# Two raw tiles of their own for the conditioning loads during the first FFN's output products

## The chip, the cores and the metric

One Trainium2 chip, one of its cores. The metric is the device time of one execution in microseconds (us); lower is better. TensorE (PE) does the matrix products, VectorE (DVE) and ScalarE (ACT) the elementwise work, GpSimd (POOL) a few reductions, SyncE (SP) issues most loads from device memory.

## The reference, cut to what matters

Two layers, S = 512 tokens, D = 1024, in float32. Each layer has a mixer and an FFN; the first layer's FFN is where this change lies.

```python
cond = jax.nn.silu(c)
for layer in range(DEPTH):
    mod = (cond @ ada_w[layer] + ada_b[layer])[:, None, :]
    sh1, sc1, g1, sh2, sc2, g2 = jnp.split(mod, 6, axis=-1)
    ...
    y = swiglu_ffn(u, ffn_w_in[layer], ffn_w_out[layer])   # (silu(gate) * up) @ w_out, w_out is 2816 x 1024
    h = h + (1.0 + g2) * rms_norm(y, norm_g[layer, 3])
```

The vector `mod` does not depend on the tokens. Its weights `ada_w` (1024 x 6144 for each layer) are read from device memory beside the FFN's own, and the kernel spreads that work over stretches in which PE is busy with something else.

## The kernel before

**Products.** A float32 operand is cut into a rounded part `hi` and a rest `lo`, and each product is three matmuls: hi by hi, hi by lo, lo by hi (`three`, lines 582, 583, 584). Weights come as float32 into a raw tile of 1 MB; ACT casts it to `hi` (line 96) and DVE subtracts to get `lo` (line 97).

**The stream.** All weights and all conditioning data go through one list of items in the order of their use (`Stream`). Each item has a kind: `"w"` (a weight to be cut), `"ada"` (1 MB of `ada_w`, which DVE multiplies by `cond` in four instructions, lines 398 and 400), `"rows"` (two 256 KB broadcasts of a bias and a gain, used at lines 447 and 448) or `"do"` (no load, only work). `fill` issues the loads of the next items, in the list's order, from the SP queue, as long as at most `raws` = 2 loaded items are not yet consumed. All of them take a tile with the tag `raw`, of which there are two, so a load waits on SP until the tile that it gets has been read for the last time, whether that was a weight or a conditioning item. SP is one queue: a load that waits holds up all behind it. `take` cuts weights up to two ahead of the one in use; three `hi`/`lo` pairs exist, so weight k can be cut once PE is done with weight k - 3.

**The first FFN's output products.** `ffn(0, ...)`: after the products by `ffn_w_in` (`seven_products`), `w_out` comes as 11 weights of 256 rows each, which this text numbers w0 to w10. One weight is two steps of 128 rows, and a step is 4 token tiles x 2 halves x 3 = 24 matmuls of 128x512. The left operand of each step is cut from the tile `mid` into `oh` and `ol` (lines 1063 and 1064, five buffers of each). Ten `ada` and two `rows` items are woven between the 11 weights. Item numbers run on through the kernel: w0, w1, w2, w3, w4, w5, w6 are `raw65`, `raw67`, `raw69`, `raw71`, `raw74`, `raw76`, `raw79`; `raw66`, `raw68`, `raw70`, `raw73`, `raw75`, ... are `ada`, `raw72` and `raw77` are `rows`. In the same stretch the rotary angles of the next layer are worked out (tiles `a0`, `a1`, `pos_i`). The steps w9 and w10 are used together, one token tile at a time, and then the next layer's attention begins.

**What sets the order.** Up to w8 the scheduler of the framework puts the instructions of each engine in an order of its own choice, from its own estimate of times; from w9 on the order is written by hand (`manual_schedule`). SP takes what the scheduler gives it.

**Sides.** Pools are stacked from the left or the right end of each partition. The tiles `th`, `tl` and `spare` of `seven_products` stand on the side opposite to `mid`; when they are given up, the pool `roll` (for `oh`, `ol`) is opened there.

Of the kernel before, what the change touches and what calls it, by code (L numbers as in the profile page):

```python
# [11 lines left out]
F32 = mybir.dt.float32  # L12
# [5 lines left out]
P = 128  # L18
# [27 lines left out]
class Stream:  # L46


    def __init__(self, nc, pool, items, raws, parts):
        self.nc, self.pool, self.items, self.raws, self.parts = nc, pool, items, raws, parts  # L50
        self.loaded = 0
        self.done = 0
        self.raw = {}
        self.ready = []
        self.wpos = [i for i, it in enumerate(items) if it[0] == "w"]
        self.taken = 0

    def _load(self, i):
        kind, src = self.items[i][:2]
        if src is None:  # L60
            self.raw[i] = None
            return
        t = self.pool.tile([P, 2048], F32, name=f"raw{i}", tag="raw", bufs=self.raws)
        if kind == "quarters":
            v = t.rearrange("p (q k b) -> p q k b", q=4, k=4)
            for k in (1, 2, 3, 0):
                self.nc.sync.dma_start(v[:, k], src[k % 2][:, k // 2 * 4:k // 2 * 4 + 4])
        elif kind == "rows":
            for k in range(2):
                self.nc.sync.dma_start(t[:, k * 512:(k + 1) * 512], src[k])  # L70
        elif isinstance(src, tuple):
            v = t.rearrange("p (s a b) -> p s a b", s=len(src), a=src[0].shape[1])
            for k, s in enumerate(src):
                self.nc.sync.dma_start(v[:, k], s)
        else:
            self.nc.sync.dma_start(t.rearrange("p (a b) -> p a b", a=src.shape[1]), src)
        self.raw[i] = t

    def fill(self, most=99):
        real = lambda i: self.items[i][1] is not None  # L80
        while self.loaded < len(self.items) and sum(map(real, range(self.done, self.loaded))) + real(self.loaded) <= self.raws:
            if most == 0:
                return
            most -= 1
            self._load(self.loaded)
            self.loaded += 1
# [212 lines left out]
def block_kernel(tc, x, c, positions, ada_w, ada_b, norm_g, hgrn_w_in, lower, hgrn_norm_g, hgrn_w_out,  # L299
                 attn_w_in, attn_w_out, ffn_w_in, ffn_w_out, inv_freq, out):  # L300
    nc = tc.nc
    act, dve, pool, pe = nc.scalar, nc.vector, nc.gpsimd, nc.tensor
# [5 lines left out]
    with ExitStack() as ctx:  # L308
# [7 lines left out]
        def bank(tag):  # L316
            uid[0] += 1
            return psum.tile([P, 512], F32, name=f"ps_{tag}{uid[0]}", tag=tag, bufs={"mm": 4, "a": 2, "b": 2}[tag])
# [248 lines left out]
        st = Stream(nc, wp, items, 2, 3)  # L567
# [453 lines left out]
        def ffn(l, first, close, nxt, side):  # L1021
            turns.close()
            close()
            with ExitStack() as fx:
# [29 lines left out]
                    seven_products(range(2 * PLAIN[l], NF), mid, pss, spare, th, tl)  # L1054
                fl.drain()
                roll = fx.enter_context(tc.tile_pool(name=f"roll{l}", bufs=1, side=bass.opposite_side(side)))
                y0 = [bank("mm") for _ in range(NT)]
                y1 = [bank("a"), bank("b"), bank("a"), bank("b")]
                parts = {}
# [32 lines left out]
                def mm(t, ks=range(4)):  # L1092
                    for k in ks:
                        prods(t, NF - 4 + k, ws[k // 2], k % 2)

                def y_steps(t):
                    n.sq_y(t, 0)
                    n.sq_y(t, 1)
                    n.gated(t, 0)
                    n.r_y(t)  # L1100
                    n.gated(t, 1)
# [24 lines left out]
                with tc.manual_schedule(engines=ORDERED):  # L1126
                    mm(0)
                    y_steps(0)
                    n.upds(0)
                    n.r_h(0)  # L1130
                    n.xn(0)
                    mm(1)
                    y_steps(1)
                    n.upds(1)
                    mm(2, (0, 1))
                    n.flip(0, [bank("mm"), bank("a")])
                    n.u_of(0, 0)
                    n.u_of(0, 1)
                    n.r_h(1)
                    n.parts_of(0, 0)  # L1140
                    n.xn(1)
                    n.parts_of(0, 1)
                    mm(3, (0, 1))
                    for hi_f, lo_f in st.pieces(2, True):
                        hi_f()
                        lo_f()
                    st.fill()
                    mm(2, (2, 3))
                    y_steps(2)
                    n.upds(2)  # L1150
                    n.flip(1, [bank("mm"), bank("b")])
                    n.u_of(1, 0)
                    n.u_of(1, 1)
                    n.r_h(2)
                    n.parts_of(1, 0)
                    n.parts_of(1, 1)
                    n.xn(2)
                    mm(3, (2, 3))
                    y_steps(3)
                    fx.close()  # L1160
                    v_prod = nxt[1]()
                    vw = [st.take(0), st.take(0)]
                    v_prod(vw, 0, range(8))
                    n.upds(3)
                    n.flip(2, [bank("mm"), bank("a")])
                    n.r_h(3)
                    n.u_of(2, 0)
                    n.u_of(2, 1)
                    n.parts_of(2, 0)
                    n.parts_of(2, 1)  # L1170
                    n.xn(3)
                    v_prod(vw, 1, range(8))
                    n.flip(3, [bank("mm"), bank("b")])
                    n.u_of(3, 0)
                    n.u_of(3, 1)
                    n.parts_of(3, 0)
                    n.parts_of(3, 1)
                    for hi_f, lo_f in st.pieces(2, True):
                        hi_f()
                        lo_f()  # L1180
                    st.fill()
                    for t in range(NT):
                        act.dma_start(h_away[t], h[:, t])
                    v_prod(vw, 2, range(8))
                    v_prod(vw, 3, range(8))
# [469 lines left out]
        def open_attention():  # L1655
# [20 lines left out]
            return v_prod  # L1676

        ffn(0, first, h0.close, ((1, 0), open_attention), "right")
        v_away = dpool.tile([P, NT, 512], F32, name="v_away")

# [644 lines left out]
        made = aux, oh, ol, [b.t for b in y0], {0: y1[0].t}, [p.t for p in ws[2:]]  # L2325
        first = mixer_out(oT, store[0], gates.pop((1, 2)).t, 1, "left", cx.close, made)
        ffn(1, first, hx.close, None, "right")


# [29 lines left out]
```

## Time and profile before

| | us |
|---|---|
| median of 3 runs | 1475.56 (1474.87 to 1476.01) |
| the profiled execution, its own time | 1476.0 |
| its span, from the first to the last instruction | 1474.1 |
| PE busy | 1430.7 |
| first product by w0 | at 523.74 |
| second step of the tail (w9, second token tile) | at 633.02 |

Times in views of the trace are counted from the span's start. An entry in square brackets behind an instruction is the idle time of its engine ahead of it and who ended it. `SPq` rows are the issues of loads, not their transfers. A busy PE entry includes the modelled end of a matmul, so two neighbours overlap: the rate is read from starts.

### The profile page before, as it was taken

The page shows a single profiled execution, that of the slowest core. Times are in us where ns is not written, and L with a number is a line of the kernel's source. Part 1 is how long each engine was busy: PE and PEld are TensorE (multiplying, and loading weights), DVE is VectorE, ACT ScalarE, POOL GpSimd, SP SyncE. Part 2 cuts the span into 40 slices and gives each one's busy share as a digit, 9 for nine tenths or more (in the row PEclk, how much of TensorE's full clock was granted, in tenths as well). Part 3 has the DMA queues.
Part 4 walks back from the last instruction along what each step waited for, and adds up shares of the span by engine and source line. Part 5 has one row for each costly group of instructions (what it writes and reads, how often), then busy time and mean ns, then how long its engine had stood idle before and what let it go on. Part 6 is the DMA issues. An engine that isn't in the chain of part 4 may idle for free. (4 is left out here: it accounts for less than half of the span.)

```text
span 1474.1 us, 25335 instructions
## 1 busy us (share of the span) xinstructions
PE 1430.7 (97%) x9903; PEld 1312.5 (89%) x9903; DVE 1113.8 (76%) x1800; ACT 824.7 (56%) x1484; POOL 190.1 (13%) x173
## 2 busy tenths in 40 slices
PE   8999999999999999998999999999999999999998
PEld 6777888889999987787998999999998999999887
DVE  4588688488888876777788877788776978887644
ACT  4434442474555542267748778657896645555332
POOL 1011102031111100231000110001012211110100
PEclk9999999999999999999999999999999999999999
DMA  9656554223333355734244543254344233334541
GB/s 308 192 192 197 172 173 145 84 78 94 110 109 111 108 178 195 230 113 143 90 122 119 147 123 109 64 172 137 94 138 149 86 104 112 110 110 149 191 143 58
DMA packets 212872, 201.10 MB, mean 136 GB/s; under 512 B 8920, under 2 KB 170640, under 8 KB 212496
## 3 DMA queue, kind: packets, MB, share of 16 engines
q1 hardware_dynamic: 209776, 192.71, 42.3%
q10 hardware_dynamic: 1952, 6.65, 1.2%
q8 instruction: 78, 1.28, 0.4%
q0 software_dynamic: 1024, 0.12, 0.2%
q14 instruction: 42, 0.34, 0.1%
HBM read 192.30 MB, written 5.30 MB: 134 GB/s over the span
## 5 line engine op out<-in xcount | busy, mean ns | idle before, releaser
L96 ACT CAST hi<-raw 128x2048 fp32r<-128x2048 f32 x41 | 78.1, 1904 | 140.7 <-DMA raw<-in_ffn_w_out_dram 82.5
L1822 PE MATMUL ps_mm<-apart,hiq 128*128 128x256 f32 (+1 forms) x608 | 137.4, 320 | 3.5 <-ACT xs L1936 2.8
L97 DVE TENSOR_TENSOR lo<-raw,hi 128x2048 fp32r<-128x2048 f32 x41 | 98.0, 2393 | 55.7 <-ACT hi L96 55.6
L582 PE MATMUL ps_mm<-uh,hi 128*128 128x512 f32 (+1 forms) x368 | 130.7, 355 | 0.0
L583 PE MATMUL ps_mm<-ul,hi 128*128 128x512 f32 (+1 forms) x368 | 128.4, 349 | 1.6 <-DVE ul L682 1.6
L584 PE MATMUL ps_mm<-uh,lo 128*128 128x512 f32 (+1 forms) x368 | 128.3, 349 | 0.0
L1822 PEld LDWEIGHTS ps_mm<-apart,hiq 128*128 128x128 f32 x608 | 99.9, 191 | 9.8 <-ACT xs L1936 3.4
L954 DVE TENSOR_TENSOR loq<-raw,hiq 128x1024 fp32r<-128x1024 f32 x72 | 85.0, 1221 | 20.2 <-ACT hiq L950 20.2
L963 PE MATMUL ps_mm<-th,hiq 128*128 128x256 f32 x360 | 99.0, 275 | 0.0
L963 PE MATMUL ps_mm<-tl,hiq 128*128 128x256 f32 x360 | 99.0, 275 | 0.0
L963 PE MATMUL ps_mm<-th,loq 128*128 128x256 f32 x360 | 99.0, 275 | 0.0
L1822 PE MATMUL ps_mm<-apart,loq 128*128 128x256 f32 (+1 forms) x304 | 95.4, 314 | 0.6 <-DVE loq L1958 0.6
L934 POOL TENSOR_TENSOR raw<-raw 128x512 f32<-128x512 f32 x36 | 47.7, 1326 | 320.1 <-DVE spare L930 165.3
L583 PE MATMUL ps_mm<-lo,oh 128*128 128x512 f32 x208 | 80.0, 385 | 5.5 <-DVE lo L97 5.4
L950 ACT CAST hiq<-raw 128x1024 fp32r<-128x1024 f32 x72 | 72.2, 1049 | 21.1 <-DVE raw L938 16.5
L582 PEld LDWEIGHTS ps_mm<-uh,hi 128*128 128x128 f32 x368 | 69.9, 190 | 12.4 <-issue 5.3
L582 PE MATMUL ps_mm<-hi,oh 128*128 128x512 f32 x208 | 79.6, 383 | 0.8 <-ACT hi L96 0.8
L583 PEld LDWEIGHTS ps_mm<-ul,hi 128*128 128x128 f32 x368 | 70.1, 190 | 9.3 <-DVE ul L682 2.0
L584 PEld LDWEIGHTS ps_mm<-uh,lo 128*128 128x128 f32 x368 | 70.0, 190 | 6.9
L1822 PE MATMUL ps_mm<-uh,hiq 128*128 128x256 f32 x256 | 72.0, 281 | 0.2 <-ACT ps_mm L1911 0.2
L1822 PE MATMUL ps_mm<-ul,hiq 128*128 128x256 f32 x256 | 71.2, 278 | 0.0
L1822 PE MATMUL ps_mm<-uh,loq 128*128 128x256 f32 x256 | 71.1, 278 | 0.0
(478 smaller groups left out, 4739.0 us busy)
## 6 DMA issues: line engine op xcount, KB each, us to landing
raw<-in_ada_w_dram SPq DMA_DIRECT2D x40, 1024.0 KB, 5.2
raw<-in_ffn_w_in_dram SPq DMA_DIRECT2D x144, 256.0 KB, 4.0
raw<-in_ffn_w_out_dram SPq DMA_DIRECT2D x22, 1024.0 KB, 4.9
raw<-in_attn_w_in_dram SPq DMA_DIRECT2D x64, 256.0 KB, 4.5
raw<-in_hgrn_w_in_dram SPq DMA_DIRECT2D x12, 1024.0 KB, 5.4
raw<-in_attn_w_in_dram SPq DMA_DIRECT2D x12, 1024.0 KB, 5.1
raw<-in_ffn_w_in_dram SPq DMA_DIRECT2D x8, 1024.0 KB, 5.0
raw<-in_attn_w_in_dram SPq DMA_DIRECT2D x16, 512.0 KB, 5.1
```

Of the source, the lines that this page charges most:

```text
L96: self.nc.scalar.copy(hi, t)
L97: self.nc.vector.tensor_sub(lo, t, hi.bitcast(F32))
L582: pe.matmul(ps, ah, bh, start=start, stop=False, skip_group_check=part)
L583: pe.matmul(ps, ah, bl, start=False, stop=False, skip_group_check=part)
L584: pe.matmul(ps, al, bh, start=False, stop=stop, skip_group_check=part)
L934: pool.tensor_add(r[:, 2], r[:, 2], r[:, 0])
L950: act.copy(hi, src)
L954: dve.tensor_sub(lo, src, hi.bitcast(F32))
L963: pe.matmul(LAID(ps), w[x][:, a], TAKE(us[kt][y]), start=begin and kt + m == 0, stop=kt == 3 and m == 2, skip_group_check=True)
L1822: pe.matmul(LAID(dst()), x, TAKE(y), start=begin and i == 0, stop=i == len(todo) - 1, skip_group_check=True)
```

## The change

While the first FFN's output products run, `ada` and `rows` items get tiles of a pool named `more`, two of them, on the side opposite to `mid`; the weights keep the two `raw` tiles for themselves. `fill` then counts weights and conditioning items apart, up to two of each, and still goes through the list in its order: it stops at the first item whose kind has no tile left. The pool is opened after `roll` and given up with it.

```diff
     def _load(self, i):
...
-        t = self.pool.tile([P, 2048], F32, name=f"raw{i}", tag="raw", bufs=self.raws)
+        if i in self.side:
+            t = self.aside.tile([P, 2048], F32, name=f"raw{i}", tag="more", bufs=2)
+        else:
+            t = self.pool.tile([P, 2048], F32, name=f"raw{i}", tag="raw", bufs=self.raws)
...
     def fill(self, most=99):
         real = lambda i: self.items[i][1] is not None
-        while self.loaded < len(self.items) and sum(map(real, range(self.done, self.loaded))) + real(self.loaded) <= self.raws:
+        while self.loaded < len(self.items):
+            i = self.loaded
+            if self.aside is not None and real(i) and self.items[i][0] in ("ada", "rows"):
+                self.side.add(i)
+            kin = sum(real(k) and (k in self.side) == (i in self.side) for k in range(self.done, i))
+            if real(i) and kin == (2 if i in self.side else self.raws):
+                self.side.discard(i)
+                return
             if most == 0:
+                self.side.discard(i)
                 return
...
                 roll = fx.enter_context(tc.tile_pool(name=f"roll{l}", bufs=1, side=bass.opposite_side(side)))
+                if l == 0:
+                    st.beside(fx.enter_context(tc.tile_pool(name="more", bufs=1, side=bass.opposite_side(side))))
+                    st.fill()
...
                     y_steps(3)
+                    st.beside(None)
                     fx.close()
```

The orders differ in this stretch alone; POOL's is the same throughout. In the rows below a line number of the changed kernel is that of before plus 9 to 21.

On SP, the loads of the first weights. `raw66` was issued before the new pool existed and still takes a `raw` tile. Before:

```order
L76 DMA raw65_4961<-in_ffn_w_out_dram 128x2x1024
L76 DMA raw66_5065<-in_ada_w_dram 128x4x512
L76 DMA raw67_5204<-in_ffn_w_out_dram 128x2x1024
L76 DMA raw68_5210<-in_ada_w_dram 128x4x512
L76 DMA raw69_5216<-in_ffn_w_out_dram 128x2x1024
L76 DMA raw70_5223<-in_ada_w_dram 128x4x512
L76 DMA raw71_5229<-in_ffn_w_out_dram 128x2x1024
L70 DMA raw72_5291<-in_ada_b_dram 128x512
L70 DMA raw72_5291<-in_norm_g_dram 128x512
L76 DMA raw73_5298<-in_ada_w_dram 128x4x512
L76 DMA raw74_5391<-in_ffn_w_out_dram 128x2x1024
```

And in the changed kernel:

```order
L85 DMA raw65_4961<-in_ffn_w_out_dram 128x2x1024
L85 DMA raw66_5065<-in_ada_w_dram 128x4x512
L85 DMA raw67_5207<-in_ffn_w_out_dram 128x2x1024
L85 DMA raw68_5209<-in_ada_w_dram 128x4x512
L85 DMA raw70_5217<-in_ada_w_dram 128x4x512
L85 DMA raw69_5215<-in_ffn_w_out_dram 128x2x1024
L85 DMA raw71_5223<-in_ffn_w_out_dram 128x2x1024
L85 DMA raw74_5299<-in_ffn_w_out_dram 128x2x1024
L79 DMA raw72_5230<-in_ada_b_dram 128x512
L79 DMA raw72_5230<-in_norm_g_dram 128x512
L85 DMA raw73_5297<-in_ada_w_dram 128x4x512
L85 DMA raw76_5398<-in_ffn_w_out_dram 128x2x1024
```

The conditioning loads `raw68` and `raw70` move ahead of w2 (`raw69`), and w2, w3 and w4 stand in a row. `raw68` waits for PE to be done with `seven_products`, whose tiles lay where `more` is.

On DVE, from the cut of w1 (`lo67`) on, with the last use of `raw66` (L400, now L417), whose tile w2 gets. Before:

```order
L856 CAST a0_5369<-pos_i_5359 32x256 x2
L400 SCALAR_TENSOR_TENSOR shared_97<-raw66_5065,cond_96,shared_97 128x512
L856 CAST a0_5369<-pos_i_5359 32x256 x2
L1064 TENSOR_TENSOR ol457_5301<-mid0_3096,oh456_5300 128x512
L97 TENSOR_TENSOR lo67_5213<-raw67_5204,hi67_5212 128x2048
L972 SCALAR_TENSOR_TENSOR mid0_3096<-shared_97 128x512
L400 SCALAR_TENSOR_TENSOR shared_97<-raw66_5065,cond_96,shared_97 128x512
L857 TENSOR_SCALAR a0_5369<-a0_5369,invf_5360 128x256
```

In the changed kernel:

```order
L1084 TENSOR_TENSOR ol457_5306<-mid0_3096,oh456_5305 128x512
L114 TENSOR_TENSOR lo67_5220<-raw67_5207,hi67_5219 128x2048
L873 CAST a0_5374<-pos_i_5364 32x256 x2
L989 SCALAR_TENSOR_TENSOR mid0_3096<-shared_97 128x512
L417 SCALAR_TENSOR_TENSOR shared_97<-raw66_5065,cond_96,shared_97 128x512
L873 CAST a0_5374<-pos_i_5364 32x256 x2
L415 TENSOR_SCALAR shared_97<-raw70_5217,cond_96 128x512
L417 SCALAR_TENSOR_TENSOR shared_97<-raw68_5209,cond_96,shared_97 128x512
```

The two pairs of casts go behind the cut of w1. Behind these rows, up to the cut of w2, stand four more rows L417, two of L1084 and three small ones of the angles.

On PE, the first products by w1 (`hi67`, `lo67`). Before:

```order
L582 MATMUL ps_mm440_5184<-hi67_5212,oh452_5231 128x512
L582 MATMUL ps_a444_5188<-hi67_5212,oh452_5231 128x512
L582 MATMUL ps_mm441_5185<-hi67_5212,oh452_5231 128x512
L582 MATMUL ps_b445_5189<-hi67_5212,oh452_5231 128x512
L582 MATMUL ps_mm442_5186<-hi67_5212,oh452_5231 128x512
L583 MATMUL ps_mm440_5184<-lo67_5213,oh452_5231 128x512
```

In the changed kernel:

```order
L599 MATMUL ps_mm440_5187<-hi67_5219,oh452_5237 128x512
L600 MATMUL ps_mm440_5187<-lo67_5220,oh452_5237 128x512
L601 MATMUL ps_mm440_5187<-hi67_5219,ol453_5238 128x512
L599 MATMUL ps_a444_5191<-hi67_5219,oh452_5237 128x512
L600 MATMUL ps_a444_5191<-lo67_5220,oh452_5237 128x512
```

Five products by `hi` stood ahead of the first one by `lo`; now it is one. In the same way eight did at w2 and four at w4, and both have one now; all other weights had one already.

More of the change, by code (lines that the diff above doesn't have):

```diff
@@ L56, in __init__, with beside @@
         self.taken = 0
+        self.aside, self.side = None, set()
+    def beside(self, pool):
+        self.aside = pool
+        assert pool is not None or not any(i in self.side for i in range(self.done, self.loaded))
     def _load(self, i):
```

## The prediction

> **What bounds the kernel now.** I read the page's first rows, then the waits of the stretch that the change touches, then PE's own rows there.
>
> ```profile
> span 1474.1 us, 25335 instructions
> PE 1430.7 (97%) x9903; PEld 1312.5 (89%) x9903; DVE 1113.8 (76%) x1800; ACT 824.7 (56%) x1484; POOL 190.1 (13%) x173
> ```
>
> PE has work nearly all the time, so a change can only win where PE idles or runs slowly. From the first product by w0 to the second step of the tail (523.74 to 633.02), the waits, with their sum, count and longest, are:
>
> ```profile
> ACT hi L96 <- DMA raw<-in_ffn_w_out_dram: 55.4, 9, 8.5
> PE ps_mm L583 <- DVE lo L97: 5.4, 4, 3.3
> PE ps_mm L582 <- ACT hi L96: 0.8, 2, 0.5
> ```
>
> ACT waits nine times for a weight's transfer, and PE waits behind it for the cut. The stretch as stages (PE busy and count first, then the other engines; behind POOL the granted clock, the share of the DMA engines, GB/s):
>
> ```profile
> 523.74:534.10 10.36, 10.36 (x51) 9.07 (x49) 10.24 (x15) 5.63 (x8) 0.00 (x0) 1.00 0.08 27
> 523.74:633.02 109.28, 103.02 (x459) 87.42 (x457) 79.16 (x120) 38.40 (x36) 16.18 (x5) 0.97 0.60 197
> 588.60:592.02 3.42, 1.48 (x6) 0.73 (x4) 2.72 (x2) 1.91 (x2) 2.71 (x1) 1.00 0.48 118
> 592.02:598.85 6.83, 5.10 (x12) 4.10 (x13) 5.75 (x16) 0.29 (x1) 0.52 (x1) 0.50 0.74 253
> 598.85:602.26 3.41, 3.41 (x17) 2.98 (x17) 1.76 (x1) 3.26 (x3) 0.00 (x0) 1.00 0.86 297
> ```
>
> The first row is w0 alone, with no wait: 48 matmuls (the count takes in neighbours at the edge) in 10.36 us, 0.2158 each. The second holds 19 steps of 24, 456 matmuls, which at that rate take 98.42. PE loses 109.28 - 98.42 = 10.86 us here. The fourth row shows part of it: after the longest wait the clock is 0.50 for 6.83 us. PE's rows where it waited:
>
> ```profile
> 546.59 0.48 PE L583 MATMUL ps_mm<-lo,oh 128*128 128x512 f32 x1 [0.24 <-DVE lo L97]
> 566.59 0.48 PE L582 MATMUL ps_mm<-hi,oh 128*128 128x512 f32 x1 [0.46 <-ACT hi L96]
> 569.24 0.48 PE L583 MATMUL ps_mm<-lo,oh 128*128 128x512 f32 x1 [1.52 <-DVE lo L97]
> 589.94 0.48 PE L582 MATMUL ps_mm<-hi,oh 128*128 128x512 f32 x1 [0.34 <-ACT hi L96]
> 593.75 0.79 PE L583 MATMUL ps_mm<-lo,oh 128*128 128x512 f32 x1 [3.33 <-DVE lo L97]
> 630.54 0.48 PE L583 MATMUL ps_mm<-lo,oh 128*128 128x512 f32 x1 [0.35 <-DVE lo L97]
> ```
>
> These are w2, w4 twice, w6 twice and w10, 6.24 us in brackets. The half clock adds 12 matmuls from 593.75 to 598.85, 5.10 - 12 x 0.2158 = 2.51. The other 2.1 is shorter waits and the run-up after each (a bracket begins only at the modelled end of the matmul before).
>
> **Why a weight is late: w6 followed back.**
>
> ```profile
> 576.24 0.69 DVE L447 TENSOR_TENSOR gate<-shared,raw 128x512 f32<-128x512 f32 x1 [2.87 <-DMA raw<-in_ada_b_dram]
> 576.85 2.28 DVE L97 TENSOR_TENSOR lo<-raw,hi 128x2048 fp32r<-128x2048 f32 x1
> 579.05 0.68 DVE L448 SCALAR_TENSOR_TENSOR gate<-gate,raw 128x512 f32<-128x512 f32 x1
> 579.16 0.38 SPq L76 DMA_DIRECT2D raw<-in_ada_w_dram  x1
> 579.76 0.38 SPq L76 DMA_DIRECT2D raw<-in_ffn_w_out_dram  x1
> 587.99 1.90 ACT L96 CAST hi<-raw 128x2048 fp32r<-128x2048 f32 x1 [8.37 <-DMA raw<-in_ffn_w_out_dram]
> 589.31 3.23 POOL L402 PARTITION_ALL_REDUCE shared<-shared  x1 [21.28 <-DVE shared L400]
> 589.92 3.78 DVE L97 TENSOR_TENSOR lo<-raw,hi 128x2048 fp32r<-128x2048 f32 x1 [0.70 <-ACT hi L96]
> ```
>
> The load of w6 gets the tile of the `rows` item, which DVE reads last at 579.05 + 0.68 = 579.73; 0.03 later SP issues it, behind an `ada` load that is 0.60 older. It lands 8.2 us after its issue, then come 1.90 of ACT and 3.78 of DVE (2.28 for the same cut where POOL was idle), and PE goes on at 593.75. DVE itself was held up by the `rows` transfer and waited with the cut of w5 (576.85). Load, cut, release and load again form one chain with the conditioning work inside.
>
> **The change part by part.** Every load, cut and product stays. *The tile that a weight waits for* is, from w3 on, that of weight k - 2, which may be cut once PE is done with k - 5; so the load of k can go out more than three weights' time ahead of its first product. Its own cut may start when PE is done with k - 3, that is 2 x 10.36 ahead, and takes 1.90 and up to 3.78. That leaves 15.0 us to spare, less what the queues take. On SP, w5 to w7 stand behind one `ada` load each (w5 and w7 behind a `rows` item too), w8 and w9 behind two. Such a load waits until DVE has used the conditioning item two before it, and DVE, in order, also does the cuts: per weight 2.28 to 3.78 for the cut, four to eight rows of about 0.7, and two of `ol`. DVE's 79.16 of work are 80% of the 98.42 that would be left: a queue that can take some us, not a bound. *The transfers* are the same bytes in 90% of the time: 197 x 109.28 / 98.42 = 219 GB/s, and 297 stands in the last stage row. I count them as hidden; without that cover the rival below prices them.
>
> *The first weights* are where the new order could be late. The rows:
>
> ```profile
> 518.68 0.37 SPq L76 DMA_DIRECT2D raw<-in_ffn_w_out_dram  x1
> 526.25 1.93 ACT L96 CAST hi<-raw 128x2048 fp32r<-128x2048 f32 x1
> 527.20 1.09 DVE L856 CAST a<-pos_i 32x256 f32<-32x256 int32 x2
> 528.32 0.75 DVE L400 SCALAR_TENSOR_TENSOR shared<-raw,cond,shared 128x512 f32<-128x512 f32 x1
> 529.11 1.03 DVE L856 CAST a<-pos_i 32x256 f32<-32x256 int32 x2
> 530.16 0.84 DVE L1064 TENSOR_TENSOR ol<-mid,oh 128x512 fp32r<-128x512 f32 x1
> 530.92 2.28 DVE L97 TENSOR_TENSOR lo<-raw,hi 128x2048 fp32r<-128x2048 f32 x1
> 533.12 0.68 DVE L972 SCALAR_TENSOR_TENSOR mid<-shared 128x512 f32<-128x512 f32 x1
> 533.23 0.37 SPq L76 DMA_DIRECT2D raw<-in_ada_w_dram  x1
> 534.49 0.37 SPq L76 DMA_DIRECT2D raw<-in_ffn_w_out_dram  x1
> 538.38 0.75 DVE L400 SCALAR_TENSOR_TENSOR shared<-raw,cond,shared 128x512 f32<-128x512 f32 x1 [0.36 <-DMA raw<-in_ada_w_dram]
> 541.78 1.90 ACT L96 CAST hi<-raw 128x2048 fp32r<-128x2048 f32 x1 [1.63 <-DMA raw<-in_ffn_w_out_dram]
> ```
>
> w1: its cut began at 530.92; the four angle casts (2.12) go behind it, so about 528.8, done at 531.1. PE wants it at 534.10 + 0.22, so the five products that used to lead are not missed. w2: behind w1's cut come two casts 1.09, `mid` 0.68 and the last use of `raw66` 0.75, so its tile is free at 533.6 and w2 is issued there, 0.9 earlier than 534.49 and now first: the `ada` loads went out when `seven_products` ended, about 523.7, ten us before. The first of two loads landed in 538.38 - 533.23 = 5.15, the second at 541.78 after 7.29. By the first, w2 lands at 538.8 and its `hi` is done at 540.7; by the second, at 542.8. DVE meanwhile has, after 533.6, two casts 1.03, one L415 and five rows L417 at 0.75 each, two of `ol` at 0.84 and three small ones at no more than a cast's 0.55: 8.9 by full durations, 8.0 by the steps between starts (530.16 to 530.92 is 0.76 for 0.84). The cut starts at 541.6 to 542.5, or 542.8 by the slower landing, and ends at 543.9 to 545.1; PE's first product by its `lo` is due at 534.10 + 10.36 + 0.22 = 544.68. So DVE, not the transfer, is likely last there, between 0.8 early and 0.4 late. I charge 0.2. If `raw70` or the angles' own small load is late behind the two new early transfers, DVE stops in front of the cut and the charge is that delay, 0 to 3.
>
> *The lead of `hi` products* goes at w1, w2 and w4. It costs nothing if the cut is there: at w1 by 3 us, at w2 as above, at w4 by the spare time. Without that cover it is 7 matmuls at w2 and 3 at w4. *The tail* (w9, w10) starts earlier by what was won; its waits on the norm's chain come from PE's own products and move with them, and all orders behind it are the same. I count that as nothing gained or lost.
>
> Sum, against the profiled execution's 1476.0: -10.86 + 0.2 = 1465.3; the median of the runs is 0.4 below that execution, so 1464.9, written as 1465.
>
> **The clock, row and rule.** Half clock follows windows in which PE was busy 1.48 of 3.42 (above) and 1.59 of 3.41, and did not follow one with 2.19:
>
> ```profile
> 1018.69:1022.10 3.41, 1.59 (x15) 1.41 (x14) 3.34 (x12) 2.38 (x6) 0.03 (x1) 1.00 0.00 0
> 1022.10:1025.51 3.41, 3.41 (x19) 3.41 (x18) 2.86 (x12) 2.56 (x5) 0.00 (x0) 0.50 0.00 0
> 834.36:837.78 3.42, 2.19 (x17) 2.13 (x18) 2.29 (x5) 3.42 (x11) 0.74 (x1) 1.00 0.00 0
> 1020.74 0.38 PE L2124 MATMUL ps_a<-qk,qk 128*128 128x128 f32 x1 [1.81 <-ACT h L2187]
> ```
>
> The wait before 1020.74 begins at 1018.93, 0.24 into the first of these windows. The stages at half clock are one or two times 3.41 long; if such windows stay where they are and the work comes 10.86 earlier (three windows and 0.63), 0.39 of the wait falls into the window before, and PE is busy 1.98 of 3.41 there. That lies between the row with half clock after it and the one without, so up to 3.41 / 2 = 1.7 less is open.
>
> [...]
>
> **The rivals.**
> 1. *w2 (or one more early weight) is late by 1.5 to 4.* For it: 0.1 to 0.8 to spare on a DVE queue with transfers in it. Against: all later weights gain time. 1.5 to 4 with up to 1.7 of half clock: 1466.5 to 1470.5.
> 2. *The later half-clock window goes too.* 1465 - 1.7, or 1463.3. For it: the 1.98 above. Against: DVE (2.86) and ACT (2.56) are nearly full in that window, so less than 1.7 may come back.
> 3. *The transfers set the pace, the change hides nothing.* Were 197 GB/s the most that they give, the stretch stays at 109.28 and the time at 1475.5. Against: 297 and 253 in the rows above.
> 4. *Slower.* DVE, not the loads, holds the cuts, so that they come as late as before, and PE no longer has its leading products at w2 and w4: (7 + 3) x 0.2158 = 2.2 more, 1477.7. It decides once the other waits give back less than 2.2; at w2 that is a cut that ends near 546.5 as before, 1.8 after it is due. Against: ahead of those late cuts it was ACT that waited for the transfer (1.63 at 541.78, 8.37 at 587.99).
>
> [...]
>
> **How the numbers follow.** Forecast 0.60 (1464 to 1466.4); rival 1 0.17; rival 2 0.15; rival 3 0.05; rival 4 0.03. Range 1462.8 to 1470, which leaves out the last two. Changes under 0.2% (2.95 us) can hardly be told from none; faster: the first three, 0.92; same 0.05; slower 0.03.
>
> **What would show it.** Right: the wait of ACT's L113 for `in_ffn_w_out` still large in sum (it is early now) but no PE wait for `lo` from w3 to w10, 456 matmuls in about 98.5 us, clock 1.00 throughout. The cut of w2 ends near 544. Wrong: a PE wait at w2 over 1 us, `ada` loads far behind the cuts, or a longer stretch after the tail's start (from 633.02 to the end 841.1 in this span) that gives the gain back.

## The result, and the profile after

The changed kernel takes 1464.45 us (median of 4 runs, 1461.9 to 1465.45), the kernel before beside it 1475.71. The ratio is 0.9918, with a 95% interval from 0.9902 to 0.9934: about 12 us faster by the ratio, 11.3 by the medians. In a second comparison it was 0.9938 (0.9922 to 0.9954), about 9 us. The forecast was 1465.0.

The profiled execution of after took 1461.9. Its first rows, then the stretch from the first product by w0 to the tail's second step in the view by stretches (the row of before that it answers to is `523.74:633.02`):

```profile
span 1460.2 us, 25343 instructions
PE 1422.7 (97%) x9903; PEld 1307.8 (90%) x9903; DVE 1119.6 (77%) x1800; ACT 825.6 (57%) x1484; POOL 196.8 (13%) x173
```

```profile
523.27:621.69 98.42, 98.42 (x459) 86.19 (x457) 86.18 (x120) 39.37 (x36) 20.89 (x5) 1.00 0.67 227
```

PE is busy in all of the 98.42 us, its clock is 1.00, and 109.28 - 98.42 = 10.86 us are gone. The waits there (in total, times, longest):

```profile
ACT oh L1083 <- PE ps_b L600: 40.6, 14, 4.3
DVE lo L114 <- ACT hi L113: 6.5, 2, 5.6
ACT hi L113 <- DMA raw<-in_ffn_w_out_dram: 5.4, 4, 2.0
```

ACT waited 55.4 for the weights' transfers before and waits 5.4 now. It waits for PE instead (first row): the order of who is late has turned round, and no row has PE as the one that waits. The transfers run at 227 GB/s where 197 were counted before.

The two profiled spans differ by 1474.1 - 1460.2 = 13.9. Of that 0.47 lies ahead of w0 (523.74 against 523.27), 10.86 in the stretch, and 2.6 behind it: from the tail's second step to the end it takes 838.5 where before took 841.1. Those 2.6 have two places. The first is the tail. Before (a row of ACT, two of DVE, then PE's transposes of the norm's result) and after:

```profile
632.57 0.60 ACT L618 ACTIVATE junk<-ps_mm 128x512 bf16<-128x512 f32 x1 [0.57 <-PE ps_mm L584]
632.54 2.29 DVE L97 TENSOR_TENSOR lo<-raw,hi 128x2048 fp32r<-128x2048 f32 x1
634.75 0.68 DVE L627 TENSOR_TENSOR yg<-ps_mm,gate 128x512 f32<-128x512 f32 x1
640.79 0.60 PE L663 MATMUL ps_mm<-ident,xn 128*128 128x128 f32 x4
656.90 0.63 PE L663 MATMUL ps_mm<-ident,xn 128*128 128x128 f32 x4 [1.25 <-DVE xn L657]
```

```profile
618.65 2.29 DVE L114 TENSOR_TENSOR lo<-raw,hi 128x2048 fp32r<-128x2048 f32 x1 [5.56 <-ACT hi L113]
621.96 0.69 DVE L644 TENSOR_TENSOR yg<-ps_mm,gate 128x512 f32<-128x512 f32 x1 [1.02 <-ACT junk L635]
629.46 0.60 PE L680 MATMUL ps_mm<-ident,xn 128*128 128x128 f32 x4
644.16 0.60 PE L680 MATMUL ps_mm<-ident,xn 128*128 128x128 f32 x4
```

Before, DVE began the cut of the first attention weight 0.48 ahead of the tail's second step (633.02), and `yg`, with which DVE's part of the norm's chain begins, came right behind it, 1.73 after that step's start; ACT's part (`junk`, the squares) had begun on time at 632.57. Now the same cut is 3.0 ahead of that step, and `yg` follows 0.27 after the step's start. From the first transpose (640.79 - 629.46 = 11.33) to the third (656.90 - 644.16 = 12.74) the changed kernel wins 1.41 more: the wait of 1.25 and the run-up behind it. The second place is the stage at half clock from 1022.10 on (a row of the prediction), which the profiled execution of after did not have; the repeat below has it again.

### The profile page after: what moved, and what is told of

Its sections match the earlier page's. It is cut to its first block, busy times and chain, and to the rows that moved or that the text cites. A ratio compares the mean times of both kernels' runs of the same rounds, so it can differ in the third digit from the quotient of the medians.

```text
span 1460.2 us, 25343 instructions
## 1 busy us (share of the span) xinstructions
PE 1422.7 (97%) x9903; PEld 1307.8 (90%) x9903; DVE 1119.6 (77%) x1800; ACT 825.6 (57%) x1484; POOL 196.8 (13%) x173
## 5 line engine op out<-in xcount | busy, mean ns | idle before, releaser
L1083 ACT CAST oh<-mid 128x512 fp32r<-128x512 f32 x44 | 37.3, 871 | 70.7 <-PE ps_b L600 62.1
```

What stands on the lines that cost most here:

```text
L1083: act.copy(PLACED(oh), SEEN(mid(f)))
```

## The experiments

The theory at the start: a weight's load waited for a tile that a conditioning item held, and on SP behind a conditioning load, so only keeping the kinds apart frees it. Rivals: the mere number of tiles; DVE's work for the conditioning, not its loads; and, for the tail, the clock.

**The changed kernel again** (no edit).

> The changed kernel once more, unchanged, as the base of the runs beside it. The theory (a weight's load no longer waits for a conditioning item's tile or behind its load on SP) puts all of the gain into two places: 10.86 us in the 19 product steps from w0 to the tail's second step, and about 1.5 us in the tail. Time 1462 to 1466, stretch 98.4 to 98.6 us. The rival, that a part of the gain of the first profiled execution was its clock (0.998 there, 0.994 to 0.995 in its other runs): then the time goes with the clock, 3.4 us of half speed per 0.0023 of clock (half of 3.41 us lost per window), and the runs at 0.994 to 0.995 lie 2 to 4 us above those at 0.998.

Measured: 1465.99 (1464.89 to 1468.42, 6 runs) against 1475.64. In its profile the stretch is 98.42 again:

```profile
522.92:621.34 98.42, 98.42 (x458) 86.19 (x457) 83.33 (x120) 39.38 (x36) 23.14 (x5) 1.00 0.67 227
```

The span is 1463.9, 3.7 longer than the first one's 1460.2. Up to 3.41 / 2 = 1.7 of that comes from one wait. In each profile PE stands still for 2.12 us at the same place, which the stages show in two neighbouring windows of the clock, after first, then the repeat (PE busy behind the first comma, clock behind POOL). A window here is 3.41 us, counted from the places where the clock changes in the same profile: from 1.00 to 0.50 and back, in after at 672.24 and 675.65, in the repeat at 1010.89 and 1014.30. Among the changes in before are 592.02, 598.85, 684.17, 687.58, 1022.10 and 1025.51, which is 2, 25, 1, 98 and 1 times 3.413 from one to the next. The rows:

```profile
1003.33:1006.74 3.41, 2.61 (x22) 2.31 (x20) 3.41 (x5) 0.39 (x1) 2.14 (x1) 1.00 0.38 112
1006.74:1010.15 3.41, 2.09 (x18) 2.09 (x19) 3.38 (x16) 3.09 (x7) 0.00 (x0) 1.00 0.01 2
1008.06 1.16 PE L2145 MATMUL ps_a<-qk,qk 128*128 128x128 f32 x8 [2.12 <-ACT h L2208]
```

```profile
1007.48:1010.89 3.41, 1.29 (x11) 1.10 (x11) 2.93 (x11) 1.56 (x4) 0.88 (x1) 1.00 0.01 2
1010.89:1014.30 3.41, 3.41 (x18) 3.41 (x18) 2.95 (x15) 3.11 (x6) 0.00 (x0) 0.50 0.00 0
1010.38 1.64 PE L2145 MATMUL ps_a<-qk,qk 128*128 128x128 f32 x8 [2.12 <-ACT h L2208]
```

In the first the wait is spread over two windows, PE is busy 2.61 and 2.09 of them, and full clock follows. In the repeat it lies whole in one, PE is busy 1.29, and the next 3.41 us run at half clock. The wait is the same; only its place in the window differs. So the loss behind it belongs to the run and not to the kernel; several such places may be why runs of one kernel differ by some us. The mean clock sorts them only in part: the two longest runs (1467.69 and 1468.42) have the lowest clock, 0.992, but 1464.89 came at 0.996 and 1466.08 at 0.997. My figure for it was also twice too large: one window of 3.41 at half clock lowers the mean by 0.5 x 3.41 / 1464 = 0.0012.

**A later `yg`.** In the tail's order of the changed kernel:

```diff
                     mm(0)
+                    for _ in range(3):
+                        dve.tensor_mul(held, y0[0], h[:, 0, 0:512])
                     y_steps(0)
```

> The changed kernel, with three more multiplications on DVE (each 128x512, about 0.6 to 0.7 us) between the tail's first products and the first yg, so that DVE comes to yg about as late as it did before the change, when it was still cutting the first attention weight there. Theory that the tail gained because DVE was free: PE's second wait for the norm returns (0.6 to 1.3 us at one or both of the xn transposes), and the kernel is 0.8 to 1.6 us slower than the changed kernel beside it. Rival, that the tail's gain was clock or chance: the three operations lie in idle time of DVE, no wait returns, 0 to 0.2 us.

```profile
623.17 2.14 DVE L1150 TENSOR_TENSOR held<-ps_mm,h 128x512 f32<-128x512 f32 x3 [0.30 <-PE ps_mm L601]
625.43 0.60 ACT L635 ACTIVATE junk<-ps_mm 128x512 bf16<-128x512 f32 x1 [4.88 <-DVE held L1150]
626.15 0.69 DVE L644 TENSOR_TENSOR yg<-ps_mm,gate 128x512 f32<-128x512 f32 x1 [0.84 <-ACT junk L635]
648.54 0.63 PE L680 MATMUL ps_mm<-ident,xn 128*128 128x128 f32 x4 [1.91 <-DVE xn L674]
PE ps_mm L680 <- DVE xn L674: 3.2, 3, 1.9
```

`yg` comes 2.5 after the second step's start (623.62) instead of 0.27, and PE's wait at the third transpose is back, 1.91 for before's 1.25; all such waits sum to 3.2, against 2.4 before and 1.1 after. From that step to the third transpose it takes 24.92, against 23.88 before and 22.47 after: 2.45 is lost, more than the 1.41 that was won. But the edit does more than hold DVE. Its three operations read the tile that ACT squares first, and ACT waited 4.88 for them (second row); in before that row of ACT was on time. So the run shows that a norm's chain which starts 2.3 later than in after costs the tail about as much. That DVE alone made it late in before is read from before's rows, `yg` directly behind the cut, and was not tested by itself. The times (1466.86 against 1465.99, with ranges of 5 and 4 us) can't tell 0.9 from nothing: here the trace carries the verdict.

**Four tiles for all.** The changed kernel with its two further tiles, but any item of the stretch takes whichever is free, in the order of the list:

```diff
-            if self.aside is not None and real(i) and self.items[i][0] in ("ada", "rows"):
+            live = [k for k in range(self.done, i) if real(k)]
+            aside = sum(k in self.side for k in live)
+            own = len(live) - aside
+            if real(i) and self.aside is not None and i < 91 and aside < 2 and (own == self.raws or aside < own):
                 self.side.add(i)
-            kin = sum(real(k) and (k in self.side) == (i in self.side) for k in range(self.done, i))
-            if real(i) and kin == (2 if i in self.side else self.raws):
-                self.side.discard(i)
+            elif real(i) and own == self.raws:
                 return
```

> The changed kernel, but the two further tiles belong to any item: four tiles in the order of the list, no separation by kind. Theory that separation by kind is what counts: a weight still waits its turn behind conditioning loads; but four tiles let it run four items ahead, so that at most a part of the 10.86 us returns, 1 to 4 us in the stretch. Rival, that the mere number of tiles counts: stretch 98.4 to 98.7 us and the time within 0.5 us of the changed kernel's.

```profile
524.89:623.31 98.42, 98.42 (x458) 86.19 (x457) 80.59 (x120) 39.01 (x36) 27.44 (x5) 1.00 0.68 227
```

No wait is left: the rival's result, and my theory's 1 to 4 us are refuted. 1467.1 (1465.28 to 1467.63) is 1.1 above the repeat's median and lies inside its range. That the kinds are kept apart is not what wins.

**One tile aside.** The changed kernel, `bufs=1` for the conditioning loads and the limit 1 for 2.

> The changed kernel with one tile for the conditioning loads in place of two. Theory that the weights' own two tiles are the whole gain: PE still has no wait in the stretch (98.4 to 98.7 us), since the conditioning items have no due time inside it; time within 0.5 us of the changed kernel's, unless the conditioning loads fall so far behind that SP, which issues in the order of the list, holds a weight behind one of them. Rival, that the second tile is needed for that reason: a conditioning load waits for DVE to release the one tile (four rows of 0.75 after a landing of about 5 us, some 8 us per item), the weight behind it on SP waits with it, and 1 to 5 us of waits return at w5 to w9.

It takes 1494.35, ratio 1.0131 (1.0112 to 1.0150): slower than before. All of it lies at the end of the stretch and in the tail, where DVE, POOL and PE read:

```profile
527.58:621.02 93.44, 93.44 (x435) 81.85 (x434) 67.73 (x91) 36.72 (x34) 17.60 (x4) 1.00 0.60 205
627.89 0.79 PE L600 MATMUL ps_mm<-lo,oh 128*128 128x512 f32 x1 [4.10 <-DVE lo L114]
636.06 0.75 DVE L417 SCALAR_TENSOR_TENSOR shared<-raw,cond,shared 128x512 f32<-128x512 f32 x1 [5.34 <-DMA raw<-in_ada_w_dram]
640.38 0.68 DVE L644 TENSOR_TENSOR yg<-ps_mm,gate 128x512 f32<-128x512 f32 x1
648.24 3.25 POOL L419 PARTITION_ALL_REDUCE shared<-shared  x1 [5.94 <-issue]
658.73 0.59 POOL L650 TENSOR_TENSOR rr<-rv,expo 128x1 f32<-128x1 f32 x1 [7.25 <-issue]
660.26 1.09 PE L680 MATMUL ps_mm<-ident,xn 128*128 128x128 f32 x4 [20.42 <-DVE xn L674]
```

For eighteen steps the weights are in time with two tiles of their own, as the theory had it (first row, PE never idle), and none of the rival's waits at w5 to w9 is there. But the time that the theory gave is missed by 28 us: the conditioning falls behind, and I had missed that it has a due time: its last rows stand ahead of the cut of w10 and of `yg` in DVE's order. PE waits 4.10 for that cut. Then DVE waits 5.34 for an `ada` transfer, `yg` follows it, POOL's reduction of the conditioning goes ahead of the norm's `rr`, and PE stands still for 20.42 us. Within these, POOL is idle for 5.94 ahead of the reduction and for 7.25 behind it, and the profile shows nothing that it waits for ("issue"); the cause of these two gaps is open. The prediction's warning, "`ada` loads far behind the cuts", would have come true here.

**Before without DVE's conditioning work.** The kernel before, two shared tiles, all loads; for the stretch's ten `ada` items DVE does one narrow operation:

```diff
-                for k in range(4):
+                if (l, v) in ((0, 5), (1, 0)) or (l, v, hf) == (1, 1, 1):
+                    if kq == 0:
+                        dve.memset(a, 0.0)
+                    dve.scalar_tensor_tensor(a[:, 0:8], r[:, 0, 0:8], cond[:, 0:1], a[:, 0:8], op0=OP.mult, op1=OP.add)
+                for k in range(0 if (l, v) in ((0, 5), (1, 0)) or (l, v, hf) == (1, 1, 1) else 4):
```

> The kernel before, with all its loads and its two shared tiles; of DVE's work on the ten ada loads of the stretch only one 8-column operation each is left (and a memset per pair), in place of four of 128x512: about 28 us less of DVE. It leaves out most of those sums of the conditioning. Theory that tiles and SP's order hold the weights: a tile comes free some 2.3 us earlier after each ada landing, but still only after that landing, and the weight's load still stands behind it; 3 to 7 of the 10.86 us remain, time 1467 to 1472. Rival, that DVE's conditioning work holds the cuts: with it gone PE's waits go, stretch 98.4 to 99.5 us, time 1463 to 1465.

**Before without the ten `ada` loads.** DVE's work stays and reads a tile that lies there:

```diff
-                r = V4(raw)
+                r = h if raw is None else V4(raw)
...
+            if (l, v) in ((0, 5), (1, 0)) or (l, v, hf) == (1, 1, 1):
+                return ("ada", None, ada_chunk(l, v, hf, kq), (l, v, hf, kq))
```

> The kernel before with its two shared tiles, without the ten ada loads of the stretch; DVE does all of its 40 operations on them, reading a tile that lies on the chip (so those sums of the conditioning are of other data). The two rows loads stay. Theory that tiles and SP's order hold the weights: with the ten loads gone only the two rows loads share the weights' tiles, the waits shrink to 0 to 2 us in the stretch, time 1464 to 1467. Rival, that DVE's conditioning work holds the cuts: it is all there, the waits of DVE's cuts remain, stretch 105 to 109 us, time 1471 to 1475.

The stretch of the first (1463.95 us), then of the second (1465.84 us) with PE's two waits at its start:

```profile
525.32:623.75 98.43, 98.43 (x459) 86.19 (x458) 58.19 (x96) 38.33 (x36) 19.23 (x5) 1.00 0.65 226
```

```profile
528.90:629.46 100.56, 98.79 (x456) 86.21 (x457) 83.37 (x117) 37.76 (x35) 17.88 (x5) 1.00 0.36 116
528.90 0.48 PE L584 MATMUL ps_mm<-hi,oh 128*128 128x512 f32 x1 [1.10 <-ACT oh L1065]
533.96 0.48 PE L584 MATMUL ps_mm<-hi,oh 128*128 128x512 f32 x1 [1.77 <-ACT shared L969]
```

Each removes all waits for weights. The two waits of the second are for other work of ACT, its `oh` and its L969; the wait of 1.10 ends where the stretch begins, so only the 1.77 and the run-up behind it are in the 100.56. In the first run the theory's 3 to 7 us are refuted and the rival's numbers came; in the second it is the other way round. Taken alone, the first would say that DVE's work was the cause, the second that the loads were. Neither is by itself: with all loads in the same two tiles and in the same order on SP the weights are in time, and with all of DVE's work too. Only both in one loop are late. The length of that loop shows in SP's issues of five weights in a row, w2 to w6, in before and in the kernel without the work (number, durations, first and last start):

```profile
L76 SPq DMA_DIRECT2D raw<-in_ffn_w_out_dram x5: 368/368/379, 534.5 to 579.8; - x5
```

```profile
L76 SPq DMA_DIRECT2D raw<-in_ffn_w_out_dram x5: 368/368/379, 533.5 to 572.8; - x5
```

Before, one of these rounds takes (579.8 - 534.5) / 4 = 11.3 us on average, and PE needs a weight every 10.36. Without DVE's work it takes (572.8 - 533.5) / 4 = 9.8. The theory was therefore changed: one loop through two tiles (landing, cuts and conditioning in DVE's order, release, next load) was 1 us too long per round. The rounds of before are not alike, though. Its next four weights, w7 to w10:

```profile
L76 SPq DMA_DIRECT2D raw<-in_ffn_w_out_dram x4: 367/368/368, 593.7 to 621.3; - x4
```

From w6 to w7 it took 593.7 - 579.8 = 13.9, and the last three rounds (621.3 - 593.7) / 3 = 9.2 each, less than PE's 10.36; there PE waited only 0.35, at w10. So the 11.3 is the mean of four early rounds and no fixed length of the loop.

**Three tiles for all**, to test that: as with four, with `aside < 1` and `bufs=1`.

> One further tile in place of two, and any item may take it: three tiles in the order of the list. Theory after the runs so far (the weights were late because one chain ran through two tiles: landing, DVE's queue, release, next load; a weight took about 12 us round this chain where PE needs one every 10.36): a third tile takes a transfer of 5 us out of the chain, so PE has no wait in the stretch, 98.4 to 98.7 us, time within 0.3% of the kernel with four shared tiles (1467.1). Rival, that two tiles must be free of conditioning items: 1 to 5 us of waits come back in the stretch, time 1468 to 1472.

```profile
526.71:632.57 105.86, 101.97 (x458) 88.24 (x457) 85.94 (x120) 38.57 (x36) 21.57 (x5) 0.97 0.63 211
583.05 0.80 PE L601 MATMUL ps_mm<-lo,oh 128*128 128x512 f32 x1 [3.29 <-DVE lo L115]
560.83 2.29 DVE L115 TENSOR_TENSOR lo<-raw,hi 128x2048 fp32r<-128x2048 f32 x1 [4.10 <-ACT hi L114]
566.37 3.52 DVE L418 SCALAR_TENSOR_TENSOR shared<-raw,cond,shared 128x512 f32<-128x512 f32 x5
569.92 0.38 SPq L85 DMA_DIRECT2D raw<-in_ffn_w_out_dram  x1
579.25 3.73 DVE L115 TENSOR_TENSOR lo<-raw,hi 128x2048 fp32r<-128x2048 f32 x1 [0.74 <-ACT hi L114]
```

1471.63 us, ratio 0.9961 (0.9947 to 0.9975): 105.86 - 98.42 = 7.4 us are lost again, at one weight. The theory's forecast of no wait is refuted, and the time lies in the rival's range; but the rival's reason, that two tiles must be free of conditioning items, does not hold either: the four shared tiles keep none free, and PE had no wait with them. My estimate of one transfer less in the loop was too kind, and no run gives a length of the loop from which the loss with three tiles could be worked out. The rows show the loop in the trace: DVE waits 4.10 with the cut of w4; the conditioning rows behind it release a tile at 569.89; 0.03 later SP issues the load of w5; its cut, slow at 3.73, ends at 582.98; PE goes on at 583.05. The mean clock of the stretch is 0.97, where it is 1.00 with four shared tiles. So of shared tiles three lose 7.4, two 10.86, four nothing.

## Why the prediction was right, and where its steps were not

*-10.86 in the stretch*: right to the hundredth, 98.42 against 98.42 in two profiles. Its reason, that transfers and DVE can be covered, held: 227 GB/s against the 219 asked for, and DVE's 86.18 of work in 98.42 without a wait of PE. *ACT's wait for the weights "still large in sum"*: wrong, 5.4. With a weight's tile no longer behind the conditioning, ACT gets its data before PE frees its places.

*+0.2 for w2*: the size is harmless, the step failed. I gave w2 the tile of `raw66`, free at 533.6.

```profile
528.14 2.32 DVE L114 TENSOR_TENSOR lo<-raw,hi 128x2048 fp32r<-128x2048 f32 x1
530.49 11.83 SPq L85 DMA_DIRECT2D raw<-in_ffn_w_out_dram  x3
535.97 1.91 ACT L113 CAST hi<-raw 128x2048 fp32r<-128x2048 f32 x1 [1.46 <-DMA raw<-in_ffn_w_out_dram]
539.64 2.28 DVE L114 TENSOR_TENSOR lo<-raw,hi 128x2048 fp32r<-128x2048 f32 x1
```

w2's load (the first of SP's three) went out at 530.49, 0.03 after w1's cut released its tile (528.14 + 2.32): w2 got the tile that came free first. In before that tile went to a conditioning load (`raw68`, issued at 533.23, 0.03 after w1's cut ended), which now has a tile of its own. The cut ended at 541.92, 2.3 before PE's first product by it in this span (523.27 + 2 x 10.36 + 0.22 = 544.21). DVE was last there, as said: `hi` was done at 537.88. Rival 1 did not happen.

*The tail "nothing gained or lost"*: the term that was left out. It gained 1.41. I argued that the norm's chain moves with PE; I did not ask what DVE had in front of `yg`, and that was the cut of the first attention weight. The rows for it stood in the profile of before.

*Rival 2*, the later stage at half clock: it went in the first profile and not in the repeat, so it is neither won nor lost by the change. My working kept the windows where they were in before; in the two profiles of the changed kernel the window around that wait begins 1.32 and 2.90 ahead of the wait's end (1008.06 - 1006.74 and 1010.38 - 1007.48). My reading, that the less busy window is the one with half clock behind it, fits these two: 2.09 of 3.41 busy was followed by full clock, 1.29 by half. But the busy share alone does not decide it. In before a window with 1.95 of 3.42 busy (223.38 to 226.80) was followed by half clock, in after one with 1.76 of 3.41 (13.46 to 16.87) by full clock. In the run with the late `yg` a stretch of 3.41 with 1.50 was followed by full clock, where 1.59 in before was followed by half:

```profile
646.12:649.53 3.41, 1.50 (x12) 1.13 (x11) 1.76 (x6) 3.38 (x10) 1.77 (x2) 1.00 0.13 49
649.53:652.95 3.42, 3.42 (x18) 2.99 (x17) 2.67 (x5) 1.61 (x6) 1.80 (x3) 1.00 0.00 0
```

So the "up to 1.7 of half clock" that rival 1 adds to a wait of 1.5 to 4 is my estimate (3.41 / 2) and no rule.

*Rivals 3 and 4* are refuted by the stretch. The total of 1464.45 is 0.6 below the forecast, and the repeat's 1465.99 is 1.0 above it. The 10.86 was understood; that the sum came so close is in part luck, since the tail's 1.41 is missing from it and the half-clock stages, which neither I nor the change could set, move a run by up to 3.41 / 2 = 1.7 for each 3.41 us, an estimate from the rows.

## What to carry to other kernels

When two kinds of loads share a ring of tiles, follow the loop from landing through every consumer's queue to the release and the next issue, and compare its rounds with the pace of the engine that must not wait: here the rounds of w2 to w6 took 11.3 in the mean against 10.36, and leaving out DVE's work, leaving out the loads or adding two tiles each ended the waits. The comparison said where to look, not how much a repair gives: one more tile was forecast to be enough and left 7.4. Taking one part away and seeing the wait go does not make that part the cause; take the other away too. And the kind that seems to have no due time gets one through an in-order queue: with a single tile for it, the last cut and `yg` stood behind it and the kernel was 28 us slower than with two.

## What the runs showed of the hardware

The same wait of 2.12 us had half clock for 3.41 us behind it in one execution and full clock in another; what differed in the rows is its place in the clock's windows. And a DVE cut of 128x2048, 2.28 us mostly, took 3.78 in before and 4.29 in after where POOL's reduction had begun 0.6 ahead of it; but in the repeat a cut that began equally far into the same reduction took 2.28, and the reduction 5.98. After, then the repeat:

```profile
595.93 3.72 POOL L419 PARTITION_ALL_REDUCE shared<-shared  x1 [8.08 <-DVE shared L417]
596.52 4.29 DVE L114 TENSOR_TENSOR lo<-raw,hi 128x2048 fp32r<-128x2048 f32 x1
```

```profile
596.63 5.98 POOL L419 PARTITION_ALL_REDUCE shared<-shared  x1 [9.06 <-DVE shared L417]
597.23 2.28 DVE L114 TENSOR_TENSOR lo<-raw,hi 128x2048 fp32r<-128x2048 f32 x1
```

With no reduction beside it a cut took 2.29 (563.74 in after), and with no cut beside it a reduction 3.23 (558.35 in after). In these rows, where the two overlap for most of the cut, at least one of them is slow. In after two others began 0.02 apart (543.48 and 543.50), and there too the reduction was the slow one, 6.50, and the cut took 2.28. What decides which one gives way was not tested.
